# First modulation in two halves of the features, with two context keys between them

## The chip, the cores and the metric

One core of a Trainium2 chip runs the kernel. The metric is the device time of one launch in microseconds (us), the median of three runs. The core's engines are TensorE (PE; PEld is its weight load), VectorE (DVE), ScalarE (ACT), GpSimd (POOL) and SyncE (SP, which issues most transfers). Each has its own instruction queue, and semaphores connect them.

## The reference, cut to what matters

A transformer block on 1024 latent rows (`x`) and 256 context rows (`ctx`), 1024 features wide. What the change touches is the first part:

```python
mod   = split(silu(c)     @ w_ada + b_ada, 6)      # sh1, sc1, g1, sh2, sc2, g2 for the latents
mod_c = split(silu(c_ctx) @ w_ada + b_ada, 6)      # the same for the context
h_lat = rmsnorm(x,   norm1_g) * (1 + sc1)  + sh1
h_ctx = rmsnorm(ctx, norm1_g) * (1 + sc1c) + sh1c
u, v, q, k, vv, r, af, ab, ga, gb = split(h @ w_in)   # for both
lf = log_sigmoid(af @ w_alpha_f + b_alpha_f) / 16     # gates, forward and backward
```

Of the context the block needs the keys `k` (4 heads of 128), the values `vv` (4 heads of 256) and the gate inputs `af`, `ab` (16 columns each). They start the gated scans of the latents. All products are in fp32, made from split operands: a high part (rounded to fp32r) and a low part (the rest), three passes each (high by high, high by low, low by high).

## The kernel before, in words

Everything before the heads' scans is written in program order, and a scheduler places it on the engines. Tiles are 128 partitions wide; `slot` tiles (40 buffers of 4 KB a partition), `raw_w` tiles (3) for loaded weights, and `wspl` tiles (4) for two split weights are reused when their readers are done. PSUM has two pools of four banks (`bank`, `gbank`).

The stages up to the gates:

1. Modulation (L309 to L361). For each of eight blocks of 128 input features, two loads of 512 KB bring `w_ada` rows for shift (`n2 = 0`) and scale (`n2 = 1`), each all 1024 features wide. `split_w` makes the high part on ScalarE (L236) and the low part on VectorE (L237); TensorE multiplies them by the four columns `cs4` (L323), into four banks `pada`, which were started with the bias (`sel` by `brow`, L312). After all 16 loads the four banks are copied to rows, transposed to columns (L353) and combined into `sh1` and `s1` (L356 to L361), for the latents (column 0) and the context (column 1).
2. Context (L343, L363). Two tiles of context rows are loaded after `w_ada`, normalised (`rms_scaled`: a square on ScalarE, two small steps on VectorE with a power on GpSimd, L172, between them, and a scaling on VectorE, L181), transposed, and scaled by `s1`, `sh1` into split operands `hc` (`modulate_T`, L194 to L196).
3. Context products. The gate inputs (`gws`, 24 products of 256 columns), then for each head a key (24) and the values (48, by two weight halves in `tm_unit`, L285). After the first head's values the latents' eight tiles are loaded and the first four are normalised, the other four two at a time behind the heads 2 and 3.
4. Latents (L402 to L403). `modulate_T` for two groups of four row tiles: per feature block four transposes (L190), a scaled high part on ScalarE, a raw value and a subtraction on VectorE (every second subtraction on GpSimd).
5. `aft`, the latents' gate inputs: 48 products of 512 columns.
6. Gates (`log_gates`, L413 on), the context's states, and the four heads.

The scheduler decides the order on each engine within this stretch; loads on SP keep the written order (`load_in_order`) up to the first three weights. `pe` (L627), which pins TensorE's order, is defined and used only behind the heads.

## Time and profile before

| | |
|---|---|
| median of three runs | 1770.04 us (1769.26 to 1771.21) |
| profiled execution | 1771.97 us |
| its span | 1770.2 us |
| TensorE busy in the span | 1712.4 us (97%) |
| VectorE, ScalarE, GpSimd busy | 1138.8, 668.5, 215.4 us |
| HBM read and written | 205.64 and 60.82 MB |

The span is what the trace covers, from the first instruction to the last. All rows below count from its start. Busy time of TensorE counts overlapping, pipelined matmuls, so a TensorE that is busy all the time is not one at its peak: the time from one matmul's start to the next one's is what a matmul costs. "Idle before" in square brackets is the engine's wait ahead of the row, with what ended it.

### The profile page before, as it was taken

What the parts mean: (1) busy time and instruction counts of PE and PEld (TensorE: products, weight loads), DVE (VectorE), ACT (ScalarE), POOL (GpSimd) and SP (SyncE); (2) the same over time, 40 slices, a digit from 0 to 9 for tenths busy, and PEclk for the clock granted to TensorE, in tenths of its full rate; (3) what the DMA queues carried; (4) which work ended last, traced back from release to release, by engine and by line L of the source; (5) the groups of instructions that cost most, each with busy time, mean ns of one, the idle gap of its engine ahead of it and who ended that gap; (6) DMA issues with size and microseconds to landing.
All of it is one profiled execution on the core that took longest, in us unless ns stands there. A gap on an engine that the chain in (4) does not pass through costs nothing.

```text
span 1770.2 us, 21603 instructions
## 1 busy us (share of the span) xinstructions
PE 1712.4 (97%) x8162; PEld 1407.5 (80%) x8162; DVE 1138.8 (64%) x1559; ACT 668.5 (38%) x974; POOL 215.4 (12%) x193
## 2 busy tenths in 40 slices
PE   8899999999899999999999999989999999999997
PEld 3887888888678888877888888768888888888886
DVE  7686595867865464277656745885545555466797
ACT  6663423323443434234322213533333333355343
POOL 2220000000112353000000000012122122000001
PEclk9999999999999999999999999989999999999999
DMA  9511234052354454387858951233222232377572
GB/s 339 156 37 36 85 118 179 24 179 60 113 155 133 129 179 125 124 293 260 262 190 308 321 191 74 70 116 98 77 90 83 75 92 84 127 242 277 180 270 99
DMA packets 219961, 267.89 MB, mean 151 GB/s; under 512 B 11920, under 2 KB 142032, under 8 KB 219856
## 3 DMA queue, kind: packets, MB, share of 16 engines
q1 hardware_dynamic: 219040, 265.08, 45.1%
q0 software_dynamic: 720, 1.40, 0.2%
q8 instruction: 64, 1.05, 0.2%
q14 instruction: 41, 0.34, 0.1%
q10 hardware_dynamic: 96, 0.02, 0.0%
HBM read 205.64 MB, written 60.82 MB: 151 GB/s over the span
## 4 chain that ended last, share of the span: by engine, by line
PE 79%; DVE 11%; DMA 4%; issue 3%; ACT 3%; POOL 1%; SPq 0%; DVEq 0%; ACTq 0%; POOLq 0%
PE m L716 20%; PE g L716 17%; PE m L273 13%; PE m L1283 5%; PE g L1283 5%; PE m L1166 5%; PE m L285 4%; PE g L538 2%; DVE s L638 1%; PE m L822 1%; DVE wlo L237 1%; DVE s L422 1%; PE g L822 1%; DMA s<-in_w_ada_dram 1%; PE g L1363 1%
## 5 line engine op out<-in xcount | busy, mean ns | idle before, releaser
L716 PE MATMUL m<-s,s 128*128 128x512 f32 x1320 | 313.5, 395 | 8.8 <-ACT q L736 3.8
L716 PEld LDWEIGHTS m<-s,s 128*128 128x128 f32 x1320 | 251.0, 191 | 65.1 <-ACT q L736 5.8
L273 PE MATMUL m<-s,whi 128*128 128x512 f32 (+1 forms) x832 | 252.3, 384 | 2.2 <-ACT s L990 1.5
L237 DVE TENSOR_TENSOR wlo<-wr,whi 128x1024 fp32r<-128x1024 f32 x92 | 112.4, 1224 | 194.2 <-ACT whi L236 194.0
L716 PE MATMUL g<-s,s 128*128 128x512 f32 x960 | 225.0, 391 | 9.0 <-ACT q L736 4.1
L716 PEld LDWEIGHTS g<-s,s 128*128 128x128 f32 x960 | 179.2, 188 | 51.6 <-ACT q L736 6.6
L273 PEld LDWEIGHTS m<-s,whi 128*128 128x128 f32 x832 | 154.0, 188 | 33.2 <-ACT s L990 2.4
L236 ACT CAST whi<-wr 128x1024 fp32r<-128x1024 f32 x92 | 96.5, 1051 | 214.1 <-PE m L273 107.9
L273 PE MATMUL m<-s,wlo 128*128 128x512 f32 (+1 forms) x416 | 158.9, 383 | 1.8 <-DVE wlo L237 1.8
L637 ACT CAST s<-s 128x1024 fp32r<-128x1024 f32 x98 | 102.4, 1052 | 134.4 <-DVE s L638 62.2
L638 DVE TENSOR_TENSOR s<-s,s 128x1024 fp32r<-128x1024 f32 x98 | 145.4, 1494 | 9.9 <-ACT s L637 6.0
L172 POOL TENSOR_TENSOR rstd<-rstd,nhalf 128x1 f32<-128x1 f32 (+2 forms) x43 | 29.1, 678 | 847.7 <-DVE rstd L171 847.6
L285 PE MATMUL m<-whi,s 128*128 128x256 f32 x640 | 126.0, 291 | 0.1
L716 PE MATMUL g<-s,whi 128*128 128x512 f32 x384 | 118.5, 390 | 0.0
L638 DVE TENSOR_TENSOR s<-wr,s 128x1024 fp32r<-128x1024 f32 x77 | 92.3, 1233 | 22.8 <-ACT s L637 22.1
L285 PEld LDWEIGHTS m<-whi,s 128*128 128x128 f32 x640 | 101.5, 192 | 4.2 <-issue 2.7
L742 POOL TENSOR_TENSOR q<-u,q 128x512 f32<-128x512 f32 x38 | 59.4, 1563 | 314.1 <-DVE u L741 150.3
L637 ACT CAST s<-wr 128x1024 fp32r<-128x1024 f32 x77 | 78.2, 1053 | 49.9 <-DMA wr<-wsT 25.3
L285 PE MATMUL m<-wlo,s 128*128 128x256 f32 x320 | 92.3, 289 | 2.6 <-DVE wlo L237 1.9
L273 PEld LDWEIGHTS m<-s,wlo 128*128 128x128 f32 x416 | 78.3, 188 | 16.6 <-DVE wlo L237 2.0
L1166 PE MATMUL m<-s,s 128*128 128x512 f32 x384 | 87.6, 390 | 0.0
L1166 PEld LDWEIGHTS m<-s,s 128*128 128x128 f32 x384 | 72.0, 188 | 14.9
(293 smaller groups left out, 2879.2 us busy)
## 6 DMA issues: line engine op xcount, KB each, us to landing
wr<-in_w_in_dram SPq DMA_DIRECT2D x82, 512.0 KB
s<-in_w_ada_dram SPq DMA_DIRECT2D x48, 512.0 KB
wr<-in_w_ffn_in_dram SPq DMA_DIRECT2D x48, 512.0 KB
wr<-actd SPq DMA_DIRECT2D x77, 256.0 KB
s<-in_w_ffn_out_dram SPq DMA_DIRECT2D x22, 512.0 KB
wsT<-s SPq DMA_DIRECT2D x44, 256.0 KB
wr<-wsT SPq DMA_DIRECT2D x44, 256.0 KB
wr<-in_w_ffn_out_dram SPq DMA_DIRECT2D x33, 256.0 KB
```

The costliest lines, as they stand in the source:

```text
L236: nc.scalar.copy(hi, raw)
L237: lo_sub[0] = nc.vector.tensor_sub(lo, raw, f(hi)).ins
L273: nc.tensor.matmul(ps, ws[a][:, k, :], get(b, k, t0, n), start=k == 0 and i == 0, stop=k == nk - 1 and i == 2)
L285: nc.tensor.matmul(ps[:, j, :], get(b, 4 * kh + k, (2 * tp + j) * P, P), ws[a][:, k, :], start=kh == 0 and j == 0 and k == 0 and i == 0, s ...
L538: r = nc.tensor.matmul(pkv[:, j, :], kt[:, j, :], vt(n), start=j == 0, stop=True, skip_group_check=True)
L637: nc.scalar.copy(hi, raw)
L638: nc.vector.tensor_sub(lo, raw, f(hi))
L716: pe(nc.tensor.matmul(ps, wts[a][:, k, :], mov[k // 2][b][:, k % 2, :], start=start and k == 0 and i == 0, stop=k == 3 and i == 2, skip_gr ...
L742: nc.gpsimd.tensor_sub(q7, u3, q7)
L822: pe(nc.tensor.matmul(banks[tt], op[mov][kp][b][:, kk, tt * P:(tt + 1) * P], wts[a][:, kk, :], start=start and kp == 0 and kk == 0 and i = ...
L1166: pe(nc.tensor.matmul(ps, yF.get(b, k, tt * P, P), wo[k // 2][a][:, k % 2, :], start=k == 0 and i == 0, stop=k == KT - 1 and i == 2))
L1283: pe(nc.tensor.matmul(banks[tt], o[b][:, 0, tt * P:(tt + 1) * P], o[a][:, 1, :], start=start and k == 0 and i == 0, stop=k == KH - 1 and i ...
```

## The change

- `w_ada` is loaded and multiplied in two halves of the output features (512 for shift and 512 for scale in each load, 8 loads for a half; `ada_rows`). After each half `columns` makes that half of `s1` and `sh1`. The bias comes as 16 more rows of `prow`, through the transpose to `pcol`, which moves ahead of the loads, and is added in `columns`. `sel`, `brow` and the four bias matmuls are gone.
- The context's rows are loaded ahead of `w_ada`. The gate weights' preparation (`wgh`, `wgt`) and their operand (`graw`, `gws`, now built on GpSimd) stand ahead of the first half.
- Between the halves the context's first four feature blocks are scaled, and the gate inputs and keys 0 and 1 are multiplied over them (`ctx_product`, 12 products each). The second halves of these three follow behind the second half of the modulation, then keys 2 and 3, then the values in eight half weights.
- The latents' eight tiles are loaded behind the first two value weights; one tile is normalised in place behind each value product. The latents' transposes stand between the last value products and around `aft`.
- Up to `aft`, TensorE's order is pinned to the written one (`mm`).

The diff, cut to its core:

```diff
+    def mm(ins):
+        return pe(ins) if pinned[0] else ins
...
+    def ada_rows(hf):
+        for k in range(KT):
+            w = slot([P, 2, 512])
+            load_in_order(w, w_ada[k * P:(k + 1) * P, 0:2048].rearrange("p (c f) -> p c f", c=2)[:, :, hf * 512:(hf + 1) * 512])
+            ws = split_w(w, [P, 2, 512], pool=True)
+            for ch in range(2):
+                for a in range(2):
+                    mm(nc.tensor.matmul(pada[2 * hf + ch], cs4[:, k, :], ws[a][:, ch, :], start=k == 0 and a == 0, stop=k == KT - 1 and a == 1))
+            yield
...
+        for ch, dst, bias in ((1, s1, bsc), (0, sh1, bsh)):
+            nc.vector.tensor_add(dst[:, ks, :], pc[:, ch, :, 2:4], both(bias))
+            nc.vector.tensor_add(dst[:, ks, :], pc[:, ch, :, 0:2], dst[:, ks, :])
+            if ch:
+                nc.vector.tensor_mul(dst[:, ks, :], dst[:, ks, :], both(n1c))
...
+    with tc.issue_after(powed[0]):
+        for d in range(2):
+            for q in range(3):
+                nc.gpsimd.tensor_copy(graw[:, :, 64 * d + 16 * q:64 * d + 16 * q + 16], gab[:, :, 16 * d:16 * d + 16])
+        gws = [slot([P, KT, P], F32R) for _ in range(2)]
+        nc.gpsimd.tensor_copy(gws[0], graw)
+        nc.gpsimd.tensor_sub(gws[1], graw, f(gws[0]))
...
+    for k, _ in enumerate(ada_rows(0)):
+        if k in (3, 6):
+            ctx_T(k // 4)
+    columns(0)
...
+    kraw = [raw_ctx(C_K + h * P) for h in range(2)]
+    mod(0)
+    done = mod(1)
...
+    ctx_product(pa[:, :TC], gws, 0)
+    kws = [split_k(r) for r in kraw]
+    ctx_product(pk[0][:, 0], kws[0], 0)
+    for k, _ in enumerate(ada_rows(1)):
+        if k == 2:
+            ctx_product(pk[0][:, 1], kws[1], 0, False)
+        if k in (4, 6):
+            ctx_T(k // 2)
+    columns(1)
+    mod(2)
+    done = mod(3)
+    ctx_product(pa[:, :TC], gws, 1)
+    aft_evac(aftc, pa[:, :TC])
+    for h in range(2):
+        ctx_product(pk[0][:, h], kws[h], 1)
+    nc.scalar.copy(kc[:, 0:2, :], pk[0])
+    kraw = [raw_ctx(C_K + h * P) for h in range(2, HEADS)]
...
+    ahead = [value_weights(i) for i in range(2)]
+    for i in range(NT):
+        xt = slot([P, D])
+        load_in_order(xt, x[i * P:(i + 1) * P, :])
+        xl.append(xt)
+    junk = slot([P, D])
+    for i in range(2 * HEADS):
...
+        if i % 2 == 1:
+            for j in range(2):
+                nc.scalar.copy(vc[j][:, i // 2, :], ps[:, j, :])
+        rms_scaled(xl[i], junk, xl[i])
+        if i + 2 < 2 * HEADS:
+            ahead.append(value_weights(i + 2))
+        if i in (4, 6, 7):
+            lat_groups(*{4: (0, 0), 6: (0, 4), 7: (4, 0)}[i])
```

Two places where the order moves. The first is VectorE between the weight tiles and the context's scaling. Before, in a row: the last four lower parts of `w_ada` (L237), the gate operand's, the two context tiles' normalisation (L171, L181), the copies and column steps, then the first key's lower part.

```order
L237 TENSOR_TENSOR s_57_282<-s_55_279,s_56_281 128x1024
L237 TENSOR_TENSOR s_60_292<-s_58_289,s_59_291 128x1024
L237 TENSOR_TENSOR s_63_302<-s_61_299,s_62_301 128x1024
L237 TENSOR_TENSOR s_66_312<-s_64_309,s_65_311 128x1024
L237 TENSOR_TENSOR s_68_320<-wr_18_151,s_67_319 128x1024
L335 COPY pcol_138<-g_69_323 128x48
L171 TENSOR_SCALAR rstd_74_333<-ss_73_331 128x1
L181 TENSOR_SCALAR s_72_330<-s_70_326,rstd_74_333 128x1024
L351 COPY s_78_344<-m_15_144 4x512
```

After, behind the first half's columns: four scalings of the context (L215, with two of the subtractions, L216), two keys' lower parts (`wlo`), and then the second half's eight tiles, of which the first two stand here.

```order
L352 TENSOR_TENSOR sh1_141<-g_55_277,sh1_141 128x8
L215 TENSOR_SCALAR raw_60_299<-g_41_227,s1_142,sh1_141 128x256
L216 TENSOR_TENSOR s_11_139<-raw_60_299,s_9_137 128x256
L215 TENSOR_SCALAR raw_61_303<-g_41_227,s1_142,sh1_141 128x256
L215 TENSOR_SCALAR raw_62_307<-g_51_262,s1_142,sh1_141 128x256
L216 TENSOR_TENSOR s_11_139<-raw_62_307,s_9_137 128x256
L215 TENSOR_SCALAR raw_63_311<-g_51_262,s1_142,sh1_141 128x256
L248 TENSOR_TENSOR wlo_69_332<-s_58_295,whi_68_331 128x1024
L248 TENSOR_TENSOR wlo_71_336<-s_59_297,whi_70_335 128x1024
L248 TENSOR_TENSOR s_74_354<-s_72_351,s_73_353 128x1024
L248 TENSOR_TENSOR s_77_364<-s_75_361,s_76_363 128x1024
```

The second half of `w_ada` now stands behind the context's scaling and two keys on the engine that makes the lower parts.

The second place is ScalarE among the context's values. Before (`s_110` to `s_116`: latent tiles; `m_103`: the first head's values; `whi_108`, `whi_131`, `whi_136`: weights), the first four squares (L179) stand ahead of the copies of the first head's values (L395):

```order
L236 CAST whi_108_534<-wr_107_532 128x1024
L179 ACTIVATE s_118_578,ss_119_579<-s_110_562 128x1024
L179 ACTIVATE s_121_585,ss_122_586<-s_111_564 128x1024
L179 ACTIVATE s_124_592,ss_125_593<-s_112_566 128x1024
L179 ACTIVATE s_127_599,ss_128_600<-s_113_568 128x1024
L395 COPY s_97_467<-m_103_501 128x256
L395 COPY s_98_468<-m_103_501 128x256
L179 ACTIVATE s_152_798,ss_153_799<-s_114_570 128x1024
L236 CAST whi_131_610<-wr_130_608 128x1024
L179 ACTIVATE s_155_805,ss_156_806<-s_115_572 128x1024
L236 CAST whi_136_643<-wr_135_641 128x1024
```

After (`s_136` to `s_140`: latent tiles; `m_145`: the first head's values; `m_107`: keys 2 and 3; `whi_131`, `whi_134`, `whi_149`, `whi_154`: value weights 0 to 3):

```order
L247 CAST whi_131_609<-wr_130_607 128x1024
L247 CAST whi_134_615<-wr_133_613 128x1024
L447 COPY s_66_317<-m_107_531 128x512
L196 ACTIVATE s_144_635,ss_146_661<-s_136_619 128x1024
L482 COPY s_112_589<-m_145_636 128x256
L482 COPY s_113_590<-m_145_636 128x256
L196 ACTIVATE s_144_635,ss_151_699<-s_137_621 128x1024
L196 ACTIVATE s_144_635,ss_157_736<-s_138_623 128x1024
L196 ACTIVATE s_144_635,ss_162_774<-s_139_625 128x1024
L247 CAST whi_149_669<-wr_148_667 128x1024
L196 ACTIVATE s_144_635,ss_168_811<-s_140_627 128x1024
L247 CAST whi_154_707<-wr_153_705 128x1024
```

The squares of the tiles 1 to 3 and the cast of value weight 2 now stand behind the copies of the first head's values, which wait for that head's last product.

## Rows read from the trace of the kernel before

**Rows 1.** The page's fourth section: shares of the chain that ended last.

```profile
PE 79%; DVE 11%; DMA 4%; issue 3%; ACT 3%; POOL 1%; SPq 0%; DVEq 0%; ACTq 0%; POOLq 0%
```

**Rows 2.** The timeline, modulation: start and duration in us, instruction, idle before.

```profile
20.49 1.05 ACT L236 CAST s<-s 128x1024 fp32r<-128x1024 f32 x1 [0.23 <-DMA s<-in_w_ada_dram]
...
28.22 1.05 ACT L236 CAST s<-s 128x1024 fp32r<-128x1024 f32 x1 [0.23 <-DMA s<-in_w_ada_dram]
...
26.23 4.62 DVE L237 TENSOR_TENSOR s<-s,s 128x1024 fp32r<-128x1024 f32 x4
...
33.52 1.27 DVE L351 COPY s<-m 4x512 f32<-4x512 f32 x2
...
37.14 0.25 DVE L361 TENSOR_TENSOR s<-s,pcol 128x8 f32<-128x8 f32 x2
...
24.13 1.09 PE L323 MATMUL m<-s,cs 128*4 128x512 f32 x4 [0.19 <-DVE s L237]
```

**Rows 3.** Lines of the gate weights: durations in ns, first and last start; and timeline.

```profile
L142 POOL DMA_DIRECT2D s<-in_w_alpha_b_dram x3: 484/484/484, 6.7 to 7.6; - x3
...
DMA to landing us min/median/max: 6.3/6.4/6.6
...
L118 POOL DMA_DIRECT2D s<-in_b_ada_dram x2: 521/585/649, 1.4 to 2.3; - x2
...
43.87 0.61 ACT L371 CAST s<-s 128x512 fp32r<-128x512 f32 x1
...
44.99 1.06 DVE L372 TENSOR_TENSOR s<-s,s 128x512 f32<-128x512 f32 x1
...
46.76 0.47 DVE L373 TENSOR_SCALAR s<-s,msk 128x512 fp32r<-128x512 f32 x1
47.27 1.11 DVE L374 SCALAR_TENSOR_TENSOR s<-s,msk,s 128x512 fp32r<-128x512 f32 x1
```

**Rows 4.** Groups by line, 30 to 106 us (busy us, mean ns); GpSimd's timeline.

```profile
L195 DVE TENSOR_SCALAR raw<-g,s,sh 128x256 f32<-128x256 f32 x8 | 4.0, 536 | 0.2 <-ACT s L194 0.2
L196 DVE TENSOR_TENSOR s<-raw,s 128x256 fp32r<-128x256 f32 x4 | 2.1, 534 | 0.1
...
41.44 0.74 POOL L196 TENSOR_TENSOR s<-raw,s 128x256 fp32r<-128x256 f32 x1 [5.95 <-DVE raw L195]
```

**Rows 5.** The chain of waits in order of time, up to 260 us: start, us, what.

```profile
69.73 2.90 PE m L273 x24
...
88.24 1.75 PE g L190 x16
...
219.45 21.79 PE m L273 x96
```

**Rows 6.** The timeline, 51 to 60 us: latent normalisations, and a weight behind them.

```profile
51.20 0.15 DVE L171 TENSOR_SCALAR rstd<-ss 128x1 f32<-128x1 f32 x1
...
52.68 0.15 DVE L171 TENSOR_SCALAR rstd<-ss 128x1 f32<-128x1 f32 x1
...
57.99 0.75 DVE L181 TENSOR_SCALAR s<-s,rstd 128x1024 f32<-128x1024 f32 x1 [0.73 <-POOL rstd L172]
58.66 1.22 DVE L237 TENSOR_TENSOR wlo<-wr,whi 128x1024 fp32r<-128x1024 f32 x1
...
55.86 1.04 ACT L236 CAST whi<-wr 128x1024 fp32r<-128x1024 f32 x1
...
54.08 1.03 PE L190 MATMUL g<-ident,s 128*128 128x128 f32 x8
...
59.93 0.39 PE L273 MATMUL m<-s,wlo 128*128 128x256 f32 x1 [1.78 <-DVE wlo L237]
```

**Rows 7.** Stretches: busy us (count) of PE, PEld, DVE, ACT, POOL; granted clock; DMA.

```profile
34.50:41.00 6.50, 6.09 (x32) 5.42 (x32) 5.36 (x14) 2.62 (x5) 0.55 (x1) 0.50 1.02 401
...
54.00:60.00 6.00, 2.73 (x21) 2.05 (x20) 3.89 (x9) 5.91 (x13) 1.64 (x3) 1.00 0.08 26
```

**Rows 8.** TensorE's timeline at the end of `aft`: the first gate product.

```profile
105.51 0.50 PE L413 MATMUL g<-s,s 64*128 64x512 f32 x1
```

More of the change, by code (lines that the diff above doesn't have):

```diff
@@ L115, in block_kernel @@
         r0 += n
-    brow = [slot([1, 1024]) for _ in range(2)]
-    for n2 in range(2):
-        nc.gpsimd.dma_start(brow[n2], b_ada[0:1, n2 * 1024:(n2 + 1) * 1024])
-    sel = cst.tile([1, 4], F32, name="sel")
-    nc.vector.memset(sel[:, 0:2], 1.0)
-    nc.vector.memset(sel[:, 2:4], 0.0)
     ones = cst.tile([P, P], F32, name="ones")
@@ L307, in rows_of @@
         return tiles
-    pada = [bank((4, 512)) for _ in range(4)]
-    for n2 in range(2):
-        for h in range(2):
-            nc.tensor.matmul(pada[2 * n2 + h], sel, brow[n2][:, h * 512:(h + 1) * 512], start=True, stop=False)
+    def ada_rows(hf):
[7 more added lines that the diff above has]
+            yield
@@ new lines, in block_kernel, with split_k, ctx_product @@
+    for k, _ in enumerate(ada_rows(0)):
+        if k in (3, 6):
+            ctx_T(k // 4)
+    columns(0)
+    def split_k(raw):
+        with tc.issue_after(done[0]), tc.issue_after(done[1]):
+            return split_w(raw, [P, KT, P])
+    def ctx_product(ps, ws, hf, start=True):
+        for k in range(4 * hf, 4 * hf + 4):
+            for i, (a, b) in enumerate(PASS):
+                mm(nc.tensor.matmul(ps, ws[a][:, k, :], hc_get(b, k, 0, TC), start=start and k == 0 and i == 0, stop=k == KT - 1 and i == 2, skip_group_check=True))
@@ new lines, in block_kernel @@
+    columns(1)
[7 more added lines that the diff above has]
+    kraw = [raw_ctx(C_K + h * P) for h in range(2, HEADS)]
+    pk = bank((P, 2, TC))
+    for h in range(2, HEADS):
+        ws = split_k(kraw[h - 2])
+        for hf in range(2):
+            ctx_product(pk[:, h - 2], ws, hf, h == 2)
+    nc.scalar.copy(kc[:, 2:4, :], pk)
@@ L406, in log_gates @@
+    aft = slot([P, T], F32R)
+    for h in range(2):
+        ps = bank()
+        mm_fm(ps, gws, hT.get, h * 512, 512)
+        aft_evac(aft[:, h * 512:(h + 1) * 512], ps)
+        if h == 0:
+            lat_groups(4, 4)
+    pinned[0] = False
     def log_gates(d, pieces):
@@ L450, in seq @@
         return slice(n * P, (n + 1) * P)
-    aft = slot([P, T], F32R)
-    for h in range(2):
-        ps = bank()
-        mm_fm(ps, gws, hT.get, h * 512, 512)
-        aft_evac(aft[:, h * 512:(h + 1) * 512], ps)
     def proj(name, n=8):
```

173 lines of the change are left out of this document (81 added, 92 removed).

## The prediction

> **What bounds the kernel now.** The chain of waits is read first: TensorE carries 79% of the span [rows 1]. TensorE time that the change frees, or adds as waiting, therefore moves the end by as much, unless a later stretch waits anyway. From the gates on (the first products that read `aft`), every engine's order is the same before and after, but for a few products at the seam. So one number decides: when does TensorE leave the last `aft` product? Before, that is at 105.5 us, where the first gate product starts, with six value products of latent head 0 already done [rows 8].
>
> TensorE's prices: 24 products of 256 columns take 2.90 us (0.12 each), 16 transposes 1.75, 96 products of 512 columns 21.8 (0.227 each) [rows 5]. From 54.08 us, where TensorE turns to the latents' first transposes [rows 6], the kernel before still has 216 products of 256 columns (25.9 us), 64 transposes (7.0), 48 products of 512 (10.9) and the six early ones (0.7): 44.5 us of work, done in 51.4. It loses 7 us to waits there. Before that it lives on the modulation: the last load is cast at 28.2, and s1 is multiplied out by 37.4 [rows 2].
>
> **The change, part by part.** I follow the new order of each engine with the durations of before.
>
> *Start.* ScalarE's queue now has the cast of the gate weights `wg` ahead of the first weight cast. Its transfers land 6.4 us after their issue; the last is issued at 7.6, and the two `b_ada` issues (1.17 us) that stood ahead are gone: 7.6 - 1.2 + 6.4 = 12.8 us [rows 3]. Cast 0.61, then VectorE's three `wgt` steps 1.06 + 0.47 + 1.11 [rows 3]: VectorE takes its first weight tile at 16.1. Eight tiles at 4.62/4 = 1.155 us [rows 2] end at 25.3, the last matmul half a burst of 1.09 later, 25.9. Loads are not late: before, the tenth 512 KB load is cast at 20.5 [rows 2], and the first half ends with the tenth.
>
> *First half's columns and scaling.* Two copies side by side (1.27/2 = 0.64), four transposes (1.75/4 = 0.44), five column steps at 0.125 and the hand-overs, estimated at 0.6 together: 2.3 us, 28.2 [rows 2, 5]. Scaling four features of the context: four raws and two subtractions on VectorE, 3.2 us with the means of 0.536 and 0.534 [rows 4], and 0.3 for the first hand-over: 31.7.
>
> *Second half.* VectorE then takes, in order, two keys' lower parts and eight weight tiles: ten times 1.155, 43.2. That is the crux: the products of the first half hide beside the second half on TensorE, but VectorE, which paces both, has no gap to fill. Matmul, columns, scaling as before: 43.8, 46.1, 49.6, GpSimd's last subtraction 0.74 [rows 4] and its products 50.7. The keys' second halves, 24 products, end at 53.6. The 36 products made early (4.3 us) are the whole gain, and s1's second half comes 8.7 us later than the whole s1 did.
>
> *Keys 2 and 3.* On ScalarE the cast of key 2 stands behind the copy of keys 0 and 1, which waits for their last product. Copy 0.6 (priced by the 0.61 cast of as many elements), cast 1.04, subtraction 1.22 [rows 3, 6]: TensorE waits 2.65 us, after two products that need no lower part. Then 96 products, 11.6 us: 67.8.
>
> *Values.* After the second value product ScalarE has two copies, the squares of latent tiles 1, 2 and 3, and only then the cast of the third value weights. VectorE has the three normalisations ahead of its subtraction. One normalisation costs VectorE 1.48 us from start to start, since it waits for GpSimd's power in the middle, 0.73 us in one of them [rows 6]. Copies 0.65, first square 1.05 and its hand-over 0.2, three times 1.48, subtraction 1.155: 7.5 us, 7.25 of them lost. Four more normalisations and two subtractions to the fifth weight are 8.2 us, against 5.5 of products: 2.5 lost more. The gain named in the title, latents loaded ahead, changes nothing here: their loads are issued as the second half's tiles set slots free, from 35 to 40 us, and are wanted from 62; their squares stand behind a copy.
>
> *Rest.* All 64 transposes and both `aft` products run nearly back to back; GpSimd's last subtraction costs 0.4. Sum: 53.6, plus work 240 x 0.12 + 7.0 + 10.9 = 46.9, waits 2.65 + 7.25 + 2.5 + 0.4 = 12.8: 113.3 us. Before, corrected for four more early products, 105.0. Later by 8.3 us.
>
> *Costed at nothing.* The four `sel` products and their bias (TensorE idles there); the bias added in VectorE's column steps instead (in the 2.3). GpSimd now builds the gate operand: six copies, a cast and a subtraction of 1024 wide, by its 0.74 for 256 columns 3.0 for the last and 5 to 8 us in all; even begun at 16 us it would be done by 24, and it is needed at 28.2; uncovered, it would cost what passes that. The 2 KB pieces of the weight loads: VectorE's pace covers them; I allow 0 to 1 us.
>
> **The clock.** Before, after a stretch in which TensorE ran only a dozen small transposes, the granted clock is 0.50 (1.2 GHz) from 34.5 to 41.0; in 54 to 60, with TensorE busy 2.7 of 6 us, it stays 1.00 [rows 7]. The new order has two such stretches of column steps. If both are followed by a slow one, the first makes TensorE the pacer of the second half: twelve key products and the four of one tile at twice their price (1.4 and, by the burst of 1.09, 0.8), in a row of work that has no gap left, +2.1. The second catches most of 24 products, 2.9 us at full pace, about +2.2. Nothing at the low end, 4.3 at the high end; I take 2.0, since the rows show one case of each. [...]
>
> **Sum.** +8.3 + 2.0 = +10.3 us. The profiled execution took 1771.97 (span 1770.20 and 1.8 around it), 1.9 over the median of the three runs; on the span 1780.5, on the median 1780.3 us.
>
> **Rivals.**
> (a) *The waits behind ScalarE's and VectorE's queues don't come, and it is faster.* Without the 12.8 us of waits TensorE leaves `aft` at 100.5, 4.5 us earlier: 1765.5 on the median. It decides at 12.8 - 8.3 = 4.5 us of waiting: below that the change wins. For it: TensorE has work enough. Against it: before, VectorE waits 0.73 for GpSimd at 57.3 with a subtraction behind it whose input was cast by 56.9, and TensorE waits 1.78 us for that subtraction [rows 6]. An engine didn't pass a waiting instruction there. [...]
> (b) *The first half goes at the pace of the loads* (the gate weights land early): the tenth load's cast at 20.5, with 1.05 and 1.155, ends at 22.7 instead of 25.3. 2.6 us off, 1777.7; with no slow clock 1775.7. Against it: the 12.8 is from rows. It doesn't cross over.
> (c) *The slow clock comes each time and also in the wait ahead of the third value weights*, where TensorE idles longest: 8.3 + 4.3, and up to 2 for that weight's products at twice their price (2.6 us), of which the wait behind them takes part: 1782.6 to 1785.
> (d) *The change doesn't do what it says*: if the first half's products didn't run beside the second, 4.3 us more, 1784.6. The new order has them there, so this is small.
>
> **Chances.** The forecast with (b), 1774 to 1782: 0.66. (c) and (d), above: 0.16. Between: waits a third smaller than counted, 1767 to 1774: 0.10. (a): 0.08. The range reaches from a little under (b) without slow clock, 1774.5, to the end of (c), 1785.0. A measurement of this kernel can tell about 0.2% (3.5 us) from no change: faster 0.07, same 0.10, slower 0.83.
>
> **What would show it.** In the profile after: VectorE without a gap from 16 to 43 us; s1's second half at 46; TensorE idle for some 7 us before the products of the third value weights, with the wait put down to the subtraction of that weight, and ScalarE's squares ahead of it; the first gate product at 112 to 117 and every later stage shifted by as much. Wrong if the gate comes before 108, if VectorE idles between the halves, or if the shift shrinks on the way to the end.

## The result, and the profile after

The changed kernel takes 1786.34 us (median of five runs, 1785.91 to 1789.37) beside 1769.26 us for the kernel before (median of five, 1767.13 to 1771.21). That is 17.1 us more, where 10.3 were forecast, and 1.3 us above the range. The measured ratio is 1.0106, 95% interval 1.0095 to 1.0118; the two medians alone give 1.0097. The profiled run of after took 1786.12 us.

Answering [rows 1], the page after: TensorE is busy for 5.3 us less than before in a span that is 14.2 us longer. It waits more.

```profile
span 1784.4 us, 21581 instructions
...
PE 1707.1 (96%) x8154; PEld 1411.7 (79%) x8154; DVE 1138.6 (64%) x1555; ACT 667.2 (37%) x971; POOL 219.6 (12%) x199
```

Answering [rows 2 to 4], the timeline after of the start and of both halves: start and duration in us, instruction, count, idle before.

```profile
13.35 1.04 POOL L368 CAST s<-wr 128x1024 fp32r<-128x1024 f32 x1
13.52 1.41 DVE L385 TENSOR_TENSOR s<-s,s 128x512 f32<-128x512 f32 x1 [1.33 <-ACT s L384]
14.47 2.67 POOL L369 TENSOR_TENSOR s<-wr,s 128x1024 fp32r<-128x1024 f32 x1
14.97 2.46 DVE L386 TENSOR_SCALAR s<-s,msk 128x512 fp32r<-128x512 f32 x1
18.13 9.16 DVE L248 TENSOR_TENSOR s<-s,s 128x1024 fp32r<-128x1024 f32 x8
35.34 2.64 DVE L248 TENSOR_TENSOR wlo<-s,whi 128x1024 fp32r<-128x1024 f32 x2 [0.39 <-ACT whi L247]
37.91 9.16 DVE L248 TENSOR_TENSOR s<-s,s 128x1024 fp32r<-128x1024 f32 x8
49.34 0.68 DVE L342 COPY s<-m 4x512 f32<-4x512 f32 x1 [2.26 <-PE m L325]
51.00 0.16 DVE L352 TENSOR_TENSOR sh<-g,sh 128x8 f32<-128x8 f32 x1
```

To be seen: the second half has VectorE's two key steps and eight weight tiles without a gap from 35.34 to 47.07 us, as forecast, and the second half of `s1` and `sh1` is complete at 51.2, where the whole `s1` was at 37.4 [rows 2]. The first tile starts at 18.13 rather than at 16.1, behind a masking step (L386) of 2.46 us, which took 0.47 before [rows 3].

In the first half TensorE is late as well. Its timeline after, and VectorE's copy of the first half's columns:

```profile
19.40 3.45 PE L325 MATMUL m<-s,cs 128*4 128x512 f32 x8 [4.33 <-DVE s L248]
22.35 2.13 PE L325 MATMUL m<-s,cs 128*4 128x512 f32 x8
...
29.10 0.68 DVE L342 COPY s<-m 4x512 f32<-4x512 f32 x1 [1.80 <-PE m L325]
```

The first eight products start 0.42 us apart, the next eight 0.25, and TensorE waits for nothing from 19.40 to the half's last product. So it falls behind VectorE at the start, at about half its later pace, and the copy waits 1.8 us behind VectorE's last tile. (The trace's record of the granted clock begins only at 22.6 us in this run, so the clock itself isn't shown there.)

Answering [rows 6], the timeline after at the third value weights:

```profile
78.47 0.65 ACT L482 COPY s<-m 128x256 f32<-128x256 f32 x2 [3.30 <-PE m L476]
79.00 1.07 ACT L196 ACTIVATE s<-s 128x1024 f32<-128x1024 f32 x1
...
82.43 1.03 ACT L247 CAST whi<-wr 128x1024 fp32r<-128x1024 f32 x1
83.51 0.80 PE L476 MATMUL m<-whi,s 128*128 128x256 f32 x2 [5.08 <-ACT whi L247]
84.63 1.22 DVE L248 TENSOR_TENSOR wlo<-wr,whi 128x1024 fp32r<-128x1024 f32 x1
85.91 0.58 PE L476 MATMUL m<-wlo,s 128*128 128x256 f32 x1 [1.60 <-DVE rstd L188]
```

The wait stands where the forecast put it: ScalarE's copies come first, the squares stand between them and the cast, and TensorE waits 5.08 + 1.60 = 6.7 us.

Answering [rows 7], four stretches after: length, then busy us (count) of PE, PEld, DVE, ACT, POOL; granted clock; DMA share; GB/s.

```profile
33.00:40.00 7.00, 6.38 (x26) 5.07 (x26) 6.58 (x8) 6.18 (x8) 1.46 (x2) 0.53 0.46 141
53.00:60.00 7.00, 6.05 (x26) 5.47 (x27) 3.05 (x6) 0.94 (x2) 1.46 (x2) 0.52 0.57 210
64.00:71.00 7.00, 6.83 (x34) 6.83 (x35) 2.12 (x3) 1.04 (x1) 0.00 (x0) 0.55 0.01 2
83.00:91.00 8.00, 5.89 (x26) 5.59 (x27) 5.29 (x11) 6.00 (x11) 2.19 (x4) 0.51 0.37 102
```

The granted clock is 0.50 of full speed for some 31 us between 25 and 120 us, in four pieces of 6.8, 6.8, 6.8 and 10.2; before it is so once in there, 34 to 41 us. Each piece begins behind or in a wait of TensorE: the columns (the longest wait 1.48 us), the columns again (1.39), the wait for key 2 (1.62 + 0.76), the wait for the third value weights (5.08 + 1.60). No row gives the clock in GHz, as the forecast does: measured are the share, 0.50, and products of 256 columns 0.213 us apart in such a piece (1.2 columns a ns), 0.12 at the full clock.

Answering [rows 8], the end of `aft` on TensorE:

```profile
118.05 4.99 PE L281 MATMUL m<-s,s 128*128 128x512 f32 x19
122.98 0.50 PE L505 MATMUL g<-s,s 64*128 64x512 f32 x1
123.75 1.31 PE L281 MATMUL m<-s,s 128*128 128x512 f32 x5
```

Five `aft` products stand behind the first gate product, so the mark to compare is the end of the last one: 125.1 us after. Before, none stands there and it is 105.6. So 19.5 us are lost up to the seam. The marks behind it keep that distance nearly to the end (19.1 at 131 us, 18.4 at 1146); then the profiled run of before meets a slow stretch of its own.

The same 24 products of TensorE before, and then after (timeline, and the stretch with columns as above):

```profile
1150.16 5.04 PE L716 MATMUL m<-s,s 128*128 128x512 f32 x14 [1.55 <-DVE u L744]
1157.85 4.63 PE L716 MATMUL m<-s,s 128*128 128x512 f32 x10 [2.65 <-DVE s L638]
...
1150.15:1163.15 13.00, 9.67 (x24) 6.85 (x24) 10.43 (x15) 4.32 (x7) 0.00 (x0) 0.64 0.40 121
```

```profile
1168.59 3.64 PE L793 MATMUL m<-s,s 128*128 128x512 f32 x14 [1.53 <-DVE u L821]
1174.72 2.56 PE L793 MATMUL m<-s,s 128*128 128x512 f32 x10 [2.48 <-DVE s L715]
...
1168.58:1177.95 9.37, 6.20 (x24) 4.25 (x24) 8.29 (x12) 4.33 (x6) 0.00 (x0) 1.00 0.39 119
```

Before, they run in part at the lower clock (0.64 in the mean) and take 13.0 us; after, at the full clock (1.00) behind waits of much the same length, 9.4. Behind this the distance is some 13.4 us, and from 1197 us on 14.2.

The two profiled runs thus end 14.2 us apart, the medians 17.1.

### The profile page after: what moved, and what is told of

Its sections match the earlier page's. It is cut to its first block, busy times and chain, and to the rows that moved or that the text cites. A ratio compares the mean times of both kernels' runs of the same rounds, so it can differ in the third digit from the quotient of the medians.

```text
span 1784.4 us, 21581 instructions
## 1 busy us (share of the span) xinstructions
PE 1707.1 (96%) x8154; PEld 1411.7 (79%) x8154; DVE 1138.6 (64%) x1555; ACT 667.2 (37%) x971; POOL 219.6 (12%) x199
## 3 DMA queue, kind: packets, MB, share of 16 engines
q0 software_dynamic: 656, 1.39, 0.3%
## 4 chain that ended last, share of the span: by engine, by line
PE 68%; DVE 6%; DMA 2%; ACT 1%; issue 1%; POOL 0%; SPq 0%; DVEq 0%; POOLq 0%; ACTq 0%
PE m L793 18%; PE g L793 17%; PE m L281 10%; PE m L1360 5%; PE g L1360 5%; PE m L1243 5%; DVE s L715 2%; PE g L899 2%; PE m L899 2%; PE g L1440 1%; PE g L1175 1%; DMA wr<-in_w_ffn_in_dram 1%; DMA s<-rd 1%; PE m L293 1%; DVE wlo L248 0%
## 5 line engine op out<-in xcount | busy, mean ns | idle before, releaser
L793 PE MATMUL m<-s,s 128*128 128x512 f32 x1320 | 308.5, 390 | 9.7 <-ACT q L813 3.8
L793 PEld LDWEIGHTS m<-s,s 128*128 128x128 f32 x1320 | 246.8, 188 | 65.1 <-ACT q L813 5.5
L281 PE MATMUL m<-s,whi 128*128 128x512 f32 x768 | 238.8, 392 | 2.9 <-ACT s L1067 2.4
L247 ACT CAST whi<-wr 128x1024 fp32r<-128x1024 f32 x88 | 92.3, 1051 | 217.7 <-PE m L281 104.8
L281 PEld LDWEIGHTS m<-s,whi 128*128 128x128 f32 x768 | 143.3, 188 | 33.8 <-ACT s L1067 3.2
L714 ACT CAST s<-s 128x1024 fp32r<-128x1024 f32 x98 | 102.5, 1052 | 130.2 <-DVE s L715 62.1
L281 PE MATMUL m<-s,wlo 128*128 128x512 f32 x384 | 149.6, 391 | 0.0
L293 PE MATMUL m<-whi,s 128*128 128x256 f32 x512 | 102.2, 292 | 0.0
L714 ACT CAST s<-wr 128x1024 fp32r<-128x1024 f32 x77 | 78.2, 1053 | 49.5 <-DVE wr L1310 19.1
L1243 PE MATMUL m<-s,s 128*128 128x512 f32 x384 | 87.6, 390 | 0.0
L293 PEld LDWEIGHTS m<-whi,s 128*128 128x128 f32 x512 | 81.3, 191 | 4.0 <-issue 2.9
L281 PEld LDWEIGHTS m<-s,wlo 128*128 128x128 f32 x384 | 72.1, 188 | 14.7
L1243 PEld LDWEIGHTS m<-s,s 128*128 128x128 f32 x384 | 71.9, 188 | 14.9
L793 PEld LDWEIGHTS g<-s,whi 128*128 128x128 f32 x384 | 72.0, 188 | 14.7
```

Of the source, the lines that this page charges most:

```text
L247: nc.scalar.copy(hi, raw)
L281: mm(nc.tensor.matmul(ps, ws[a][:, k, :], get(b, k, t0, n), start=k == 0 and i == 0, stop=k == nk - 1 and i == 2))
L293: mm(nc.tensor.matmul(ps[:, j, :], get(b, 4 * kh + k, (2 * tp + j) * P, P), ws[a][:, k, :], start=kh == 0 and j == 0 and k == 0 and i == 0 ...
L714: nc.scalar.copy(hi, raw)
L793: pe(nc.tensor.matmul(ps, wts[a][:, k, :], mov[k // 2][b][:, k % 2, :], start=start and k == 0 and i == 0, stop=k == 3 and i == 2, skip_gr ...
L1243: pe(nc.tensor.matmul(ps, yF.get(b, k, tt * P, P), wo[k // 2][a][:, k % 2, :], start=k == 0 and i == 0, stop=k == KT - 1 and i == 2))
```

## The experiments

All edits are to the changed kernel, but for one. "End" is the end of the last `aft` product in the run's profile; ratio and median are those of the timed runs, beside runs of the kernel before on the same chip.

| run | edit | end, us | median, us | ratio to before (95%) |
|---|---|---|---|---|
| before | | 105.6 | 1769.26 | 1 |
| after | | 125.1 | 1786.34 | 1.0106 (1.0095 to 1.0118) |
| e1_fill | short fills of TensorE's idle time | 120.8 | 1784.03 | 1.0094 (1.0079 to 1.0109) |
| e7_fill_all | long fills | 120.1 | 1783.45 | 1.0091 (1.0077 to 1.0105) |
| e3_operand_off | gate operand off GpSimd | 123.3 | 1787.54 | 1.0113 (1.01 to 1.0126) |
| e5_wgt_late | gate weights prepared ahead of `aft` | 124.1 | 1788.73 | 1.0124 (1.0106 to 1.0142) |
| e6_kcopy | key copy behind the next casts | 120.7 | 1781.88 | 1.0084 (1.0067 to 1.01) |
| e2_values | latents' squares out of the values' way | 119.3 | 1781.18 | 1.0079 (1.0063 to 1.0094) |
| e4_whole | halves undone | 119.6 | 1785.84 | 1.0097 (1.0078 to 1.0116) |
| e12_unpinned | TensorE's order free | 116.9 | 1782.99 | 1.0081 (1.0067 to 1.0096) |
| e15_whole_unpinned | e4 and e12 together | 117.5 | 1780.03 | 1.0072 (1.0057 to 1.0087) |
| e8_repaired | e2 (four tiles ahead), e5, e6 together | 112.6 | 1779.37 | 1.0065 (1.0052 to 1.0079) |
| e9_whole_repaired | e8 and e4 | 111.3 | 1774.68 | 1.0041 (1.0028 to 1.0054) |
| e13_halves_free | e8, e3, gate weights behind the context's gate inputs, order free | 109.8 | 1774.06 | 1.004 (1.0026 to 1.0054) |
| e14_whole_free | e13 and e4, key loads later | 107.5 | 1771.09 | 1.0021 (1.0013 to 1.003) |
| e10_best | e9, e3, gate weights behind the context's gate inputs, key loads later, a fill | 108.5 | 1769.6 | 1.0013 (1.0005 to 1.0022) |
| e11_before_fill | the kernel before, with a fill | 105.6 | 1768.73 | 1.0004 (0.9995 to 1.0013) |

The end in a profile and the median agree only within some us: in e4 the profiled run took 1780.0, the other three 1785.7 to 1787.7. Where a step below is sized from ends, it is so for the profiled runs. The runs were also on different chips: the kernel before has medians from 1767.1 to 1769.3 us beside them, so medians of different rows compare to some 2 us only.

### Is it the clock?

Products of 512 columns on data at hand, into a bank that nothing reads, keep TensorE busy behind both halves' columns, ahead of keys 2 and 3, and ahead of the third value weights (e1: 7, 7, 8, 20; e7: 18, 18, 8, 28).

```diff
+    def fill(n):
+        fb = gbank()
+        for _ in range(n):
+            mm(nc.tensor.matmul(fb, scanm[:, :P], scanm, start=True, stop=True))
     columns(0)
+    fill(7)
     columns(1)
+    fill(7)
```

> The changed kernel with idle-time products added on TensorE that nobody reads: 7 behind the column steps of each half, 8 ahead of key 2, 20 ahead of the third value weights (512 columns each, 1.6, 1.6, 1.8 and 4.5 us at the full clock). Waits of the other engines stay as they are. Theory A (the 7 us that the forecast missed are mostly the granted clock, 0.50 in four stretches at 33-39, 54-60, 64-70 and 81-90 us, some 10 us in all): the clock stays at or near 1.00 there, the first gate product comes at 113 to 116 instead of 123.0, time 1776 to 1779. Theory B (the time is in the waits, the clock only goes along): the gate product moves by less than 3 us, 1783 or more. If only some stretches stay at 1.00, each gives back 1.6 to 3.2 us.

e1 still has three slow stretches, shorter ones of 3.4 us each; its end is 4.2 us earlier. So the longer fills:

```diff
     columns(0)
+    fill(18)
...
+        if i == 2:
+            fill(28)
```

> As the first kernel with idle-time products, but with enough of them to reach over the context's scaling too: 18 behind the column steps of each half (4.1 us), 8 ahead of key 2, 28 ahead of the third value weights. Theory A (a gap in TensorE's work of some microseconds is what the slow stretches follow): no stretch at 0.50 between 30 and 120 us, first gate product at 112.5 to 115 instead of 123.0 (118.7 with the shorter fill), time 1776 to 1779. Theory B (the slow stretches come by chance or from something else): some of them stay, gate product at 117 or later.

Now the same four stretches of e7_fill_all are at the full clock (columns as above):

```profile
33.00:40.00 7.00, 6.17 (x37) 4.91 (x35) 6.37 (x9) 5.78 (x8) 1.48 (x2) 1.00 0.29 92
53.00:60.00 7.00, 6.78 (x46) 6.09 (x45) 3.87 (x8) 1.76 (x4) 1.47 (x2) 1.00 0.72 273
64.00:71.00 7.00, 7.00 (x61) 7.00 (x60) 2.54 (x3) 2.90 (x4) 0.00 (x0) 1.00 0.16 43
83.00:91.00 8.00, 7.24 (x60) 7.04 (x59) 5.74 (x10) 4.91 (x9) 1.75 (x4) 1.00 0.52 143
```

And its timeline, VectorE at the second half, TensorE at the end of `aft`:

```profile
36.37 2.65 DVE L248 TENSOR_TENSOR wlo<-s,whi 128x1024 fp32r<-128x1024 f32 x2 [0.39 <-ACT whi L247]
...
50.33 0.68 DVE L342 COPY s<-m 4x512 f32<-4x512 f32 x1 [2.23 <-PE m L325]
...
118.77 1.30 PE L281 MATMUL m<-s,s 128*128 128x512 f32 x5
```

From the key's lower part to the copy of the second half's columns: 13.96 us here (36.37 to 50.33), 14.00 after (35.34 to 49.34). **The first slow stretch costs nothing**: VectorE paces it. From that copy to the end of `aft`: 69.7 us here, 75.7 after. **The other three cost 6.0 us** (by the marks of keys 0 and 1, of keys 2 and 3, and of `aft`: 1.7, 2.7 and 1.5). The 10 us that theory A gave the clock are too many, and the forecast's 2.0 too few. So theory A holds for the stretches and not for the price: the first gate product comes at 118.0, not at 112.5 to 115. The timed runs hardly show it: the medians differ by 2.9 us, but by only 0.8 when each is taken above the kernel before on its own chip, and the intervals overlap. e7 has short slow stretches elsewhere, at 23 to 27, 146 to 150 and 1166 to 1170 us, which after has not. The 6.0 is thus shown in the profiled runs alone.

The same fill in the kernel before, where `s1` is multiplied out:

```diff
+    fb = gbank()
+    with tc.issue_after(ada_mm.ins):
+        for _ in range(9):
+            nc.tensor.matmul(fb, scanm[:, :P], scanm, start=True, stop=True)
```

> The kernel before with 9 idle-time products on TensorE (512 columns each, 2 us) while it waits for the copies of the modulation's rows. If the slow stretch of 34-41 us follows that wait and TensorE is on the path there: the clock stays at 1.00, the first gate product comes 2 to 3 us earlier than 105.5, time 0.1 to 0.2% below the kernel before. If VectorE's scaling paces that stretch anyway: no change.

```profile
34.50:41.00 6.50, 4.15 (x35) 3.43 (x35) 5.52 (x14) 2.79 (x6) 0.55 (x1) 1.00 1.00 380
59.50:63.50 4.00, 3.71 (x18) 3.71 (x19) 2.54 (x6) 1.31 (x4) 1.10 (x2) 0.57 0.49 132
```

In the windows of e11_before_fill the slow stretch of [rows 7] is gone, the first gate product is where it was (105.53), and another stretch, which before had at the full clock, is slow. The time doesn't change. That isn't only the new stretch taking back what the old one gave: the latents' first transposes, which come between the two, start at 53.92 instead of 54.08, so the old stretch was worth 0.16 us. Here, as in the first stretch of after, VectorE was the pacer, and the slow clock had no price.

### GpSimd's operand and the gate weights

```diff
-        nc.gpsimd.tensor_copy(gws[0], graw)
-        nc.gpsimd.tensor_sub(gws[1], graw, f(gws[0]))
...
     columns(0)
+    nc.scalar.copy(gws[0], graw)
+    nc.vector.tensor_sub(gws[1], graw, f(gws[0]))
```

> The changed kernel with the gate operand's cast and subtraction taken off GpSimd: ScalarE casts and VectorE subtracts behind the first half's columns; GpSimd keeps the six small copies. Theory A (GpSimd's work and VectorE's delay each other while both run): VectorE's step with one tensor and one scalar takes 0.5 us instead of 2.46, its first weight tile starts at 16.2 instead of 18.1, the eight tiles stay at 1.15 each and end at 25.4 instead of 27.3; with 1.2 us for the moved subtraction the last product of the latents' gate inputs comes 1 to 2 us earlier than 125.0. Rival (the long step is VectorE's own or a wait for data): still 2.4 us, first tile at 18.1.

VectorE's timeline of e3_operand_off:

```profile
13.19 0.69 DVE L383 TENSOR_TENSOR s<-s,s 128x512 f32<-128x512 f32 x1 [1.04 <-ACT s L382]
13.92 0.49 DVE L384 TENSOR_SCALAR s<-s,msk 128x512 fp32r<-128x512 f32 x1
...
15.11 9.16 DVE L248 TENSOR_TENSOR s<-s,s 128x1024 fp32r<-128x1024 f32 x8
...
28.57 1.21 DVE L404 TENSOR_TENSOR s<-wr,s 128x1024 fp32r<-128x1024 f32 x1
```

The two gate-weight steps take 0.69 and 0.49 instead of 1.41 and 2.46, and the first tile starts 3.0 us earlier. So "costed at nothing" was wrong: GpSimd was done in time, but it held VectorE up. The gain doesn't carry through: TensorE again starts at about half pace (2 or 3 products touch each half us from 16.5 to 22.5, 3 to 6 behind it), so that the copy of the first columns waits 3.0 us for it (27.31 instead of 29.10), the subtraction, now VectorE's, takes another 1.2, and the second columns' copy starts only 0.6 earlier (48.73 instead of 49.34). In this run the slow stretches behind the waits for key 2 and for the third value weights are 3.4 us shorter each, and the end comes 1.8 earlier; the timed runs don't show it.

e7's fills happen to shift GpSimd by a little, so that its steps meet the weight tiles instead (timelines of GpSimd and VectorE):

```profile
15.61 1.91 POOL L368 CAST s<-wr 128x1024 fp32r<-128x1024 f32 x1
17.60 3.23 POOL L369 TENSOR_TENSOR s<-wr,s 128x1024 fp32r<-128x1024 f32 x1
```

```profile
16.54 2.05 DVE L248 TENSOR_TENSOR s<-s,s 128x1024 fp32r<-128x1024 f32 x1
...
18.52 3.40 DVE L248 TENSOR_TENSOR s<-s,s 128x1024 fp32r<-128x1024 f32 x1
```

Both tiles end 1.1 us after the GpSimd step that was running when they began (18.59 after 17.52, 21.92 after 20.83), which is a tile's own time (1.145): by these times they made no headway until it was done. L386 after looks alike: the subtraction ends at 17.14, L386 at 17.43. But 0.29 us is less than its own 0.49, so it was held up for all but its last part. That one engine stands still while the other's step lasts fits the tiles (3.40 us instead of 1.22). It fits GpSimd's subtraction less well: held until the second tile's end (18.59) and then 2.67 long, it would end at 21.26, and it ended at 20.83. By what the two engines hold each other up no run shows. The rows of before had a trace of all this: the first of the gate-weight steps, 1.06 us in [rows 3], began while GpSimd was at a subtraction (44.76 to 45.50), and takes 0.69 in e3.

Then the gate weights' preparation just ahead of `aft`:

```diff
-    wgh = slot([P, 512], F32R)
-    nc.scalar.copy(wgh, wg)
...
+    wgh = slot([P, 512], F32R)
+    nc.scalar.copy(wgh, wg)
```

> The changed kernel with the gate weights' preparation (the cast and VectorE's three steps that stood ahead of the first weight tile) moved to just ahead of the latents' gate inputs. VectorE then takes its first weight tile when the first cast is done, near 12 us instead of 18.1, and the first half ends with its loads, near 23.2 instead of 27.3. Theory A (the start is on the path): the first gate product at 119 instead of 123.0, time 1782 on the scale on which the changed kernel has 1786. Rival (a later wait takes it up): less than 1.5 us. VectorE's step with one tensor and one scalar, 2.46 us in the changed kernel and 0.47 before, should be back at some 0.5 when it runs late, where GpSimd has no such work.

```profile
13.75 11.08 DVE L248 TENSOR_TENSOR s<-s,s 128x1024 fp32r<-128x1024 f32 x7 [0.68 <-ACT s L247]
```

In e5_wgt_late seven tiles take 11.08 us, 1.58 each instead of 1.145, beside GpSimd's cast and subtraction, which now run from 14.00 to 19.21. These seven start 4.4 us earlier than the eight of after (18.13), the first gate product (118.5) comes 4.5 earlier, but at the seam VectorE has three steps more (2.2 us) ahead of the last scalings, `aft` ends only 0.9 earlier, and the time is no better. The masking step, expected at some 0.5 us there, takes 0.69 in this run and 0.49 in e9, which has the same move.

### The two queues of ScalarE

In both, ScalarE's and VectorE's orders are pinned in that stretch so that the scheduler can't put them back. First, the copy of keys 0 and 1 behind the casts of keys 2 and 3:

```diff
-    nc.scalar.copy(kc[:, 0:2, :], pk[0])
...
+    kws = [split_k(r) for r in kraw]
+    inorder(0, nc.scalar.copy(kc[:, 0:2, :], pk0))
```

> The changed kernel with the copy of keys 0 and 1 put behind the casts of keys 2 and 3 on ScalarE; nothing else moves. The waits of 1.6 and 0.8 us ahead of key 2 should go. Theory A: without them the clock holds at 1.00 in 64-70 us as well (3.2 us more): 5.6 us, gate product at 117.4, time 1780.7. If the slow clock comes there all the same: 2.4 us, 1784. Rival (the next wait takes it up): within 1 us of 1786.

The wait for key 2 and the slow stretch behind it go together, and the end comes 4.3 us earlier. The window 64 to 71 of e6_kcopy:

```profile
64.00:71.00 7.00, 7.00 (x61) 7.00 (x60) 2.70 (x4) 3.63 (x5) 0.00 (x0) 1.00 0.28 77
```

Second, latent tiles 0 to 2 normalised ahead of the value weights, and each cast ahead of copies and squares:

```diff
+    for i in range(3):
+        rms_scaled(xl[i], junk, xl[i])
+    ahead = [split_w(raw, [P, 4, 256]) for raw in ahead]
...
+        if i + 2 < 2 * HEADS:
+            ahead.append(split_w(value_raw(i + 2), [P, 4, 256]))
```

> The changed kernel with ScalarE's and VectorE's order changed among the values alone: latent tiles 0 to 2 are normalised ahead of the value weights, and the cast and subtraction of each further value weight stand ahead of the copies and of the next square. The waits ahead of the third value weights (5.1 and 1.6 us) should go. Theory A: the slow clock of 81-90 us goes with them (2.3 us more): first gate product at 114, time 1777. Theory B (clock a by-product without a price): 6.7 us, 1779.6. Rival C (the waits move on to a later weight or to the latents' transposes): less than 4 us, 1782 or more.

The waits at the third and fifth value weights are gone, and the end comes 5.8 us earlier. A part is lost again: the latents' transposes now wait for VectorE (the waits of e2_values, us in all, times, longest), and a slow stretch follows at 102.5 to 106 (eight transposes take 1.97 us there, 1.37 at 99.5).

```profile
PE g L216 <- DVE raw L224: 2.1, 2, 1.8
```

### Halves or pin?

```diff
-    mod(0)
-    done = mod(1)
...
-    ctx_product(pa[:, :TC], gws, 0)
...
     for k, _ in enumerate(ada_rows(1)):
...
+    mod(0)
+    mod(1)
+    ctx_T(3)
...
+    ctx_product(pa[:, :TC], gws, 0)
```

> The changed kernel without what stands between the halves: the second half of the weight tiles follows the first half's columns directly, and all of the context's scaling, the gate inputs and keys 0 and 1 come behind the second half's columns. Loads, pinned order and everything behind keys 0 and 1 are as in the changed kernel. Theory A (the two halves themselves cost, since VectorE paces both and the key weights and scaling stand in its row): VectorE's 16 tiles end near 38 instead of 47.1, the second columns at 41.5, keys 0 and 1 end at 53 to 56 instead of 61.3; 5 to 8 us less, time 1778 to 1781. Rival (the 36 products made early are a net gain, 4.3 us): 1789 to 1791.

```diff
-    pinned = [True]
+    pinned = [False]
```

> The changed kernel without the pin on TensorE's order; loads and source order stay. VectorE's order up to the second half's columns and ScalarE's up to the third value weights come out the same, TensorE's differs by some transposes and by gate and key products that stand in a row by feature. Theory A (VectorE's and ScalarE's rows set the time, TensorE's pin little): last product of the latents' gate inputs at 121 to 126 (125.0 with the pin), 1783 to 1787. Rival (the pin is what costs): 115 or less, 1777 or less.

Both lines together, the halves undone and the order free:

```diff
-    pinned = [True]
+    pinned = [False]
...
-    ctx_product(pa[:, :TC], gws, 0)
...
+    mod(0)
+    mod(1)
```

> The changed kernel without the halves and without the pin, nothing repaired. Without the pin alone the last product of the latents' gate inputs came at 116.9, without the halves alone at 119.6, 125.0 with both. Theory H (halves and pin cost separately): 111 to 113. Rival (one of them only uncovers the other's wait): 115 to 117.

Undoing the halves alone takes 5.5 us off the end (of a profile that is faster than e4's other runs), the pin alone 8.1, both 7.6. By the ends the two don't add. The medians (1785.84, 1782.99, 1780.03) are too scattered to say whether they do. VectorE's copy of the second columns in e12_unpinned:

```profile
47.58 0.68 DVE L342 COPY s<-m 4x512 f32<-4x512 f32 x1 [0.72 <-PE m L325]
```

It waits 0.72 us behind VectorE's last tile instead of 2.26, since TensorE no longer has to take context transposes and key 1's products ahead of a tile that is ready. (At the full clock of e7 it was 2.23: the pin, not the clock, makes this tail.)

Then with the waits repaired: e5, e6 and e2 together, four tiles ahead.

```diff
+    for i in range(4):
+        rms_scaled(xl[i], junk, xl[i])
...
+        if i < 4:
+            rms_scaled(xl[4 + i], junk, xl[4 + i])
```

> The changed kernel with the three orders repaired together: gate weights' preparation late, the copy of keys 0 and 1 behind the casts of keys 2 and 3, four latent tiles normalised ahead of the value weights and each further weight's cast and subtraction ahead of the copies and the next square. The two halves stay. Alone the parts gave or should give 4.1, 4.3 and 5.8 to 9 us: first gate product at 106 to 109 instead of 123.0 (105.5 in the kernel before). If the parts overlap it is later than 110. Time: 0.0 to 0.2% above the kernel before.

The same with e4's edit:

```diff
-    mod(0)
-    done = mod(1)
...
+    mod(0)
+    mod(1)
+    ctx_T(3)
```

> The repaired kernel with the halves undone as well: the second half of the modulation follows the first directly, all scaling of the context and the products behind it. Theory A (the halves cost, because VectorE paces both): first gate product 3 to 6 us earlier than in the repaired kernel with the halves, 101 to 104, and with that up to 4 us earlier than in the kernel before: time 0 to 0.25% below it. Rival (with the waits repaired, the 36 products beside the second half are a gain): 2 to 4 us later than the repaired kernel with the halves.

And both with TensorE's order free, the operand off GpSimd and the gate weights prepared behind the context's gate inputs, e13 with halves, e14 without. e14 differs from e13 in one thing more: with no work between the halves, the keys are loaded behind all of `w_ada`.

```diff
-    pinned = [True]
+    pinned = [False]
...
+    nc.scalar.copy(gws[0], graw)
+    nc.vector.tensor_sub(gws[1], graw, f(gws[0]))
```

> The two halves with every repair (gate operand off GpSimd in the ring, gate weights behind the context's gate inputs, copy of keys 0 and 1 and squares behind the weight casts) and without the pin on TensorE's order. Theory P (the pin's 8 us and the repairs of ScalarE's and VectorE's rows are the same time, told twice): last product of the latents' gate inputs at 107 to 111, little better than the repaired kernel with the pin (112.6 less 3 for GpSimd). Theory Q (they add): 105 or less. In the kernel before it is at 105.6.

```diff
+    kraw = [raw_ctx(C_K + h * P) for h in range(2)]
+    columns(1)
...
-    kraw = [raw_ctx(C_K + h * P) for h in range(2)]
...
-    ctx_product(pk[0][:, 0], kws[0], 0)
...
+        for hf in range(2):
+            ctx_product(pk[0][:, h], kws[h], hf, h == 0)
```

> The whole modulation with every repair, keys' weights loaded behind w_ada, without the pin and without idle-time products. Theory H (the halves themselves cost, VectorE being the pacer): 2 to 4 us earlier than the halves with the same repairs, last product of the latents' gate inputs at 103 to 107, time 0.1% below to 0.1% above the kernel before. Rival (with TensorE free the 36 products beside the second half pay): as late as the halves or later.

Repairs bring the end from 125.1 to 112.6 (e8), and with the free order, the operand off GpSimd and the gate weights moved to 109.8 (e13). With the waits repaired the halves cost 1.3 us at the end (e8 to e9); e13 to e14 is 2.3, but includes the later key loads. The medians of these pairs differ by 4.7 and 3.0. With nothing repaired and the order free the halves end 0.6 earlier (e12 beside e15), by the medians 3.0 later. So no pair of medians shows them as a gain, and what they cost is known to a few us only.

The last run seeks a version that is better than before: e9 with the keys loaded behind all of `w_ada`, the operand off GpSimd, the gate weights behind the context's gate inputs, and one fill.

```diff
+    kraw = [raw_ctx(C_K + h * P) for h in range(2)]
+    columns(1)
+    fill(8)
+    mod(0)
+    mod(1)
+    ctx_T(3)
```

> The kernel with the whole modulation and repaired orders once more changed: the two keys' weights are loaded behind w_ada, the gate operand's cast and subtraction are off GpSimd, the gate weights are prepared behind the context's gate inputs, and 8 idle-time products stand behind the second half's columns. The last product of the latents' gate inputs came at 111.3 in the kernel it starts from (105.5 in the kernel before). Loads 2.6 us, VectorE's tiles beside GpSimd up to 2, the slow clock of 42-52 us up to 5, VectorE's 2.4 us of gate weights away from the end: 102 to 106, time 0 to 0.2% below the kernel before. If the gains overlap: 107 to 109, 0.1 to 0.25% above.

It ends at 1.0013 (1.0005 to 1.0022). No version passed the kernel before. In that kernel's trace the scheduler's order already mixes gate inputs, the first key and the first values feature by feature (39 to 50 us), so TensorE has work there without halves; that this is why none passed it is argued, not shown.

## Why the prediction was right in sign and too small

The steps that failed are two terms of the sum: GpSimd's work, costed at nothing, and the slow clock, taken at 2.0 us with the wait for key 2 left out of it. GpSimd delayed VectorE's first tile by 3.0 us, and the slow stretches cost 6.0 at the end of `aft`; the tails behind VectorE's last tiles came on top.

Right, by its own steps:

- *What bounds it.* The end of `aft` decides, and the loss there reaches far: 19.5 us there, 18.4 still at 1146 us. Over all runs the median, taken above the kernel before on its own chip, follows the end of `aft` within -2.4 to +5.2 us, so the end is a good mark, but no measurement to 1 us.
- *The crux.* VectorE paces the second half without a gap, and the products hidden beside it on TensorE are no gain at the end (e4, e9 and e14 have none of them and no later median).
- *Where the waits stand and what they cost.* Third value weights 6.7 us (7.25 forecast), key 2 2.4 (2.65). The fifth is 0.3 (2.5 forecast):

```profile
92.94 1.22 DVE L248 TENSOR_TENSOR wlo<-wr,whi 128x1024 fp32r<-128x1024 f32 x1
...
94.22 0.38 PE L476 MATMUL m<-wlo,s 128*128 128x256 f32 x1
```

  VectorE needs 8.3 us from the third lower part to the fifth (85.85 to 94.16), as forecast. But TensorE's products of the third and fourth weights, the first of them at a granted clock of 0.50, take from 85.91 to 94.08, 8.2 us instead of the 5.5 of the forecast: the slow products stand where the wait would have been. So the two terms can't be added. (In e7, at the full clock, VectorE has one normalisation less ahead of that lower part, and the wait is 0.76.) Rival (a), that these waits don't come, is out.
- *Latents loaded ahead.* They change nothing: their loads are early enough even for e2, which squares three of them before the values.
- *Rival (d).* Key products do run inside the second half; it falls.

Wrong, in the order of the path:

- *"Costed at nothing": GpSimd.* The time GpSimd needs was right (5.6 us), that it costs nobody anything was not. VectorE's first tile comes at 18.13 instead of 16.1: +2.0; by e3 the interference is 3.0, as the forecast without it was itself 1.0 too late.
- *Columns, scaling and tails*, +3.1 in all up to the second columns: from VectorE's last tile to its copy of the columns it is 1.8 and 2.3 us, where the forecast has 0.6, and the first scaling takes 0.9 more; the column steps themselves are 0.4 shorter each. The first tail goes with TensorE's half pace at the start of the half (0.42 us a product, then 0.25), which the forecast hadn't. e12 shows that the second tail comes from the pin.
- *The clock, taken at 2.0 with 4.3 as its end:* 6.0 by e7. The forecast laid its price on the two column steps. The first costs nothing (2.1 forecast) and the second 1.7 (2.2). The stretch behind the wait for the third value weights (1.5) was left to rival (c), and the one behind the wait for key 2, the dearest (2.7), stood in no term and no rival. The row 54 to 60 of [rows 7], full clock beside a half-busy TensorE, was the ground for 2.0 instead of 4.3; one row at the full clock was too little for that. Rival (c) was nearest in mechanism, and its 1782.6 to 1785 still lacks the two terms above. In the trace after the clock is at 0.50 behind all four waits named above, and three of the four cost time. It isn't so behind every wait: those of 1.5 and 2.5 us at 1167 to 1175 us in the same trace have the full clock (1.00) behind them.
- *The shift carries one to one.* Not quite: the profiles end 14.2 apart, since that of before has the slow stretch at 1150 to 1168, and the medians 17.1. "If the shift shrinks on the way to the end" was one of the forecast's signs of being wrong; it came, by a clock that differs between two runs, not by a wait.

In sum at the end of `aft`, against the forecast without its clock (113.3, measured 125.1): GpSimd 2.0, columns and tails 3.1, clock 6.0 are 11.1 of 11.8 us. The rest, 0.7, is what is left of pieces of either sign that weren't all followed: the second scaling is 0.7 longer than forecast, and the waits are shorter, in part because of the slow clock that is counted in the 6.0. That the time came only 1.3 us above the range is luck in part: the upper end was rival (c)'s sum, which has neither GpSimd nor the tails nor the stretch behind key 2, and the 19.5 us lost up to the seam had become 17.1 in the medians.

What stays open: why slow stretches come late in one run and not in the next of the same kernel (before at 1150 us, e4's runs 1780 and 1786 to 1788). No run here tells.

## What to carry to other kernels

Splitting a stage so that TensorE can start early is worth nothing while another engine paces the stage and the split puts that engine's remaining work later; ask when the last input of the stage is ready, not when the first is. Pinning an order that a scheduler had filled with whatever was ready turns late operands into waits, and behind the four named here came a slow clock (0.50) on top, 6.0 us of price in all by e7: cost a new wait on TensorE with its slow stretch, and leave that out only where another engine is the pacer or another wait takes its place. Work given to an idle GpSimd was not free here, with VectorE running beside it: it delayed VectorE's first tile by 3.0 us.

## What the runs showed of the hardware

- In e7 two weight tiles on VectorE that began while a GpSimd step ran ended 1.1 us after that step, 2.05 and 3.40 us long instead of 1.22; after, the masking step L386 took 2.46 instead of 0.49. GpSimd's steps beside VectorE's tiles were longer as well in e7 (cast 1.91 instead of 1.04, subtraction 3.23 instead of 2.67).
- With the fill in the kernel before, the slow stretch of 34 to 41 us is gone (1.00 instead of 0.50) and another stands at about 60 to 63 us (0.57 in the mean from 59.5 to 63.5, instead of 1.00), with no change in time. Whether the one follows from the other no run shows.
- Three slow stretches of 6.8, 6.8 and 10.2 us cost 1.7, 2.7 and 1.5 us. Products 0.213 instead of 0.12 us apart all through them would lose 3.0, 3.0 and 4.5, an estimate. In the last, the slow products stand where a wait was forecast.
- Waits of 1.5 and 2.5 us had a slow stretch behind them in one profiled run (before, 1150 to 1168 us, 0.62 in the mean) and none in another with the same products (after, 1169 to 1178, 1.00).
